# Two feed-forwards of a transformer: the up projections by seven block products in place of eight

## The chip, the cores and the metric

One core of a Trainium2 chip runs the whole kernel. The metric is the device time of one execution in microseconds (us), the median of several runs. A core has five engines that work side by side, each through its own list of instructions in order: TensorE (PE: matmuls into PSUM, with a weight load PEld ahead of each), VectorE (DVE), ScalarE (ACT), GpSimd (POOL) and SyncE (SP, which issues most loads from memory here). They wait for one another by semaphores.

## The reference

A model of two layers over 512 latent and 256 context tokens of width 1024, in float32. Layer 0 mixes by attention, layer 1 by a gated recurrent scan (HGRN); after each mixer comes a feed-forward. Layer 0's runs over all 768 tokens, layer 1's over the 512 latent ones only.

```python
def modulate(h, shift, scale):
    return h * (1.0 + scale) + shift

def swiglu(h, w_in, w_out):          # w_in 1024 x 5632, w_out 2816 x 1024
    a, u = jnp.split(h @ w_in, 2, axis=-1)
    return (jax.nn.silu(a) * u) @ w_out

# per layer; shift, scale and gate come from ada_w[i], six chunks of 1024 columns
h = h + gt1_l * mixer(modulate(rms_norm(h, norm_mix_w[i]), sh1_l, sc1_l))
h = h + gt2_l * swiglu(modulate(rms_norm(h, norm_ffn_w[i]), sh2_l, sc2_l), ffn_w_in[i], ffn_w_out[i])
```

## The kernel before

Tokens stand in the columns, features in the 128 partitions: `hT` is eight tiles of 128 x 768. Every float32 product is done in three passes of a rounded format (`mm3`): `split` makes of each operand a rounded high part (a cast on ACT) and the rest as a low part (a subtraction on VectorE, in a few places on POOL); TensorE then does high by high, high by low and low by high into the same PSUM tile.

A feed-forward (`ffn`) goes through the 2816 hidden features in 22 pairs of tiles: 128 columns of the a half and 128 of the u half of `w_in`. For each, `chain` loads a raw weight tile (128 x 1024, 512 KB, four buffers `raw`), splits it into `whi` and `wlo` (three buffers each), and runs eight contraction tiles by three passes over the tokens: in layer 0 a matmul of 512 and one of 258 columns each time, in layer 1 one of 256 and one of 258. The two extra columns carry the modulation's shift, for the tokens go in not yet normalised: only `hT` times a column `a_c` is split into `fnh` and `fnl`. Each token's reciprocal root of its mean square (`rst`) is found meanwhile by `token_scale`, and multiplied into the product afterwards by `scaled`, which reads PSUM and writes `ta` or `tu`; `hidden` then makes silu(a) x u of them and splits it into `gh` and `gl`. After 8, 7 and 7 pairs (`PARTS`) the down projection runs over what is there and adds the result to `hT` (`residual`, the `hT<-ffo` operations).

The reciprocal root: squares on ACT are added up, `rstd_cols` sums them over the features by small matmuls and takes the power -1/2 on POOL, `rstd_psum` turns the columns into a row in PSUM, by diagonal blocks `dg` on VectorE and a matmul that broadcasts.

Between these steps `fill.step` puts pieces of other work: the modulation of a later stage (`ada_ffn`, `ada_acc`), which multiplies weight rows by the conditioning vector on VectorE (`adacc<-adw`) while it streams 512 KB tiles. In layer 0 that is chunk 5 of layer 0, then all six of layer 1. The order of each engine's list is fixed when the program is built, by the order in which the code is written and by a scheduler of the framework; at run time engines only wait.

The stages of the profiled execution: preparation to about 184 us, attention to 437.5, feed-forward 0 from 439 to about 1019, the scan to about 1497, feed-forward 1 to the end.

## Time and profile before

| | us |
|---|---|
| median of 3 runs (1899.4 to 1904.18) | 1900.67 |
| profiled execution | 1901.45 |
| its span | 1899.4 |
| TensorE busy | 1833.4 (97%) |
| VectorE busy | 1127.6 (59%) |
| ScalarE busy | 680.3 (36%) |
| GpSimd busy | 394.8 (21%) |

The mean granted TensorE clock was 0.988 of full speed. In the rows of the profile, L106 is line 106 of the kernel; `out<-in` names the tiles an instruction writes and reads; `<-` behind a number of idle time names who ended the wait. Groups give the busy total, the mean duration in ns, and the idle time ahead of them. Rows of a timeline begin with the start and the duration.

### The profile page before, as it was taken

Reading aid. Unit: us, or ns where it says so; the run is one execution under the profiler, and the core shown is the slowest. Engines: PE = TensorE matmul, PEld = TensorE weight load, DVE = VectorE, ACT = ScalarE, POOL = GpSimd, SP = SyncE. Lnnn points to the kernel's source line nnn. Section 1 sums busy time; section 2 is a strip of 40 time slices with the busy share of each in tenths; the row PEclk is TensorE's granted clock in tenths of the full one; section 3 lists DMA queues with packets and bytes.
Section 4 is the critical chain, followed back from the end, with each engine's and each line's share of the span. In section 5 each row is a group of like instructions: output and inputs, shape, how many; then the busy total and the mean of one; then the engine's idle time right before and its main releaser. Section 6 shows DMA issues by size and latency. Waiting matters only on the chain. (4 is left out here: it accounts for less than half of the span.)

```text
span 1899.4 us, 29674 instructions
## 1 busy us (share of the span) xinstructions
PE 1833.4 (97%) x12111; PEld 1633.3 (86%) x12111; DVE 1127.6 (59%) x1821; ACT 680.3 (36%) x1222; POOL 394.8 (21%) x401
## 2 busy tenths in 40 slices
PE   8989999998999999999998989999998999999998
PEld 6778788887888888888887979889897799898997
DVE  3676788888866446445545555564647744344444
ACT  3333877763321122112224423233333432222224
POOL 1243534532000000000002444354436100000000
PEclk9989999998999999999999999999999999999999
DMA  9433200012424235353321211111111133333331
GB/s 325 169 104 100 100 2 23 23 46 78 155 89 133 79 93 174 88 154 107 100 66 51 79 45 45 57 56 56 56 56 45 45 93 97 89 89 98 92 88 57
DMA packets 206152, 166.37 MB, mean 88 GB/s; under 512 B 6801, under 2 KB 189249, under 8 KB 206017
## 3 DMA queue, kind: packets, MB, share of 16 engines
q1 hardware_dynamic: 205728, 163.43, 28.1%
q8 instruction: 96, 1.57, 0.3%
q10 hardware_dynamic: 288, 1.05, 0.1%
q14 instruction: 40, 0.32, 0.1%
HBM read 162.36 MB, written 2.10 MB: 87 GB/s over the span
## 5 line engine op out<-in xcount | busy, mean ns | idle before, releaser
L106 PE MATMUL ffi<-fnl,whi_fi 128*128 128x258 f32 (+2 forms) x1408 | 439.5, 312 | 2.6 <-DVE fnl L781 2.6
L105 PE MATMUL ffi<-fnh,whi_fi 128*128 128x258 f32 (+2 forms) x1408 | 440.3, 313 | 1.4 <-ACT fnh L780 1.3
L107 PE MATMUL ffi<-fnh,wlo_fi 128*128 128x258 f32 (+2 forms) x1408 | 437.5, 311 | 0.0
L106 PEld LDWEIGHTS ffi<-fnl,whi_fi 128*128 128x128 f32 x1408 | 268.2, 190 | 19.3 <-DVE fnl L781 3.6
L105 PEld LDWEIGHTS ffi<-fnh,whi_fi 128*128 128x128 f32 x1408 | 266.8, 190 | 18.0 <-ACT fnh L780 1.5
L107 PEld LDWEIGHTS ffi<-fnh,wlo_fi 128*128 128x128 f32 x1408 | 267.2, 190 | 15.9
L82 ACT CAST whi_fi<-raw_fi 128x1024 fp32r<-128x1024 f32 x88 | 92.3, 1050 | 359.0 <-issue 190.3
L250 POOL TENSOR_TENSOR rc<-rc,mhalf 128x2 f32<-128x2 f32 (+2 forms) x6 | 6.4, 1068 | 929.0 <-DVE rc L248 929.0
L105 PE MATMUL ffo<-gh,whi_fo 128*128 128x512 f32 (+1 forms) x542 | 192.2, 355 | 0.9 <-DVE modc L206 0.5
L107 PE MATMUL ffo<-gh,wlo_fo 128*128 128x512 f32 (+1 forms) x542 | 190.8, 352 | 0.0
L106 PE MATMUL ffo<-gl,whi_fo 128*128 128x512 f32 (+1 forms) x542 | 190.7, 352 | 0.0
L646 DVE SCALAR_TENSOR_TENSOR hT<-ffo,modc,hT 128x512 f32<-128x512 f32 (+1 forms) x74 | 47.8, 648 | 128.7 <-PE ffo L107 128.6
L222 DVE SCALAR_TENSOR_TENSOR adacc<-adw,csil,adacc 128x1024 f32<-128x1024 f32 x70 | 88.3, 1280 | 57.5 <-DMA adw<-in_ada_w_dram 57.3
L82 ACT CAST whi_fo<-raw_fo 128x896 fp32r<-128x896 f32 (+1 forms) x48 | 47.0, 980 | 202.5 <-PE ffo L106 98.5
L105 PEld LDWEIGHTS ffo<-gh,whi_fo 128*128 128x128 f32 x542 | 101.9, 188 | 16.8 <-issue 1.5
L106 PEld LDWEIGHTS ffo<-gl,whi_fo 128*128 128x128 f32 x542 | 101.9, 188 | 15.4
L107 PEld LDWEIGHTS ffo<-gh,wlo_fo 128*128 128x128 f32 x542 | 101.8, 188 | 15.3
L1103 POOL TENSOR_TENSOR KD<-KD,tot 128x384 f32<-128x384 f32 x96 | 100.3, 1068 | 68.7 <-ACT kc L1086 67.1
L85 DVE TENSOR_TENSOR wlo_fi<-raw_fi,whi_fi 128x1024 fp32r<-128x1024 f32 x87 | 106.1, 1221 | 7.5 <-ACT whi_fi L82 6.5
L660 POOL TENSOR_SCALAR pf<-pf,st 128x768 f32<-128x768 f32 (+1 forms) x96 | 73.7, 769 | 119.3 <-DVE st L659 75.5
L85 DVE TENSOR_TENSOR ptl<-pt,pth 128x384 fp32r<-128x384 f32 (+1 forms) x160 | 79.5, 522 | 9.7 <-ACT pth L82 8.4
L1103 DVE TENSOR_TENSOR QD<-QD,tot 128x256 f32<-128x256 f32 x96 | 56.3, 626 | 42.2 <-PE lv L1096 42.0
(315 smaller groups left out, 4203.2 us busy)
## 6 DMA issues: line engine op xcount, KB each, us to landing
raw_fi<-in_ffn_w_in_dram SPq DMA_DIRECT2D x88, 512.0 KB, 3.8
adw<-in_ada_w_dram SPq DMA_DIRECT2D x80, 512.0 KB, 4.3
raw_fo<-in_ffn_w_out_dram SPq DMA_DIRECT2D x32, 448.0 KB, 3.6
raw_fo<-in_ffn_w_out_dram SPq DMA_DIRECT2D x16, 512.0 KB, 3.8
raw_hz<-in_hgrn_w_in_dram SPq DMA_DIRECT2D x14, 512.0 KB, 3.8
adr<-in_ada_w_dram SPq DMA_DIRECT2D x16, 256.0 KB, 4.5
adr<-in_ada_w_dram SPq DMA_DIRECT2D x8, 512.0 KB, 7.0
raw_wq<-in_attn_w_qkv_dram SPq DMA_DIRECT2D x8, 512.0 KB, 5.5
```

The source lines that it names most:

```text
L82: ACT.copy(hi, src)
L85: (eng or DVE).tensor_tensor(lo, src, hi.bitcast(F32), op=ALU.subtract)
L105: PE.matmul(ps, ahi, bhi, start=first, stop=False)
L106: PE.matmul(ps, ahi, blo, start=False, stop=False)
L107: PE.matmul(ps, alo, bhi, start=False, stop=last)
L222: DVE.scalar_tensor_tensor(a, raw, cc, a, op0=ALU.mult, op1=ALU.add)
L250: POOL.tensor_tensor(rc, rc, mhalf.to_broadcast([P, nt]), op=ALU.pow)
L646: DVE.scalar_tensor_tensor(hT[o][:, a:e], ps, mcol(layer, ch, o, v), hT[o][:, a:e], op0=ALU.mult, op1=ALU.add)
L660: POOL.tensor_scalar(pf, pf, st3[:, 2:3], 1.0, op0=ALU.mult, op1=ALU.mult)
L1103: eng.tensor_tensor(view, view, f, op=ALU.mult)
```

## The change

With the features of w_in split into two halves of 512, the a and u tiles of a pair form a 2 x 2 block matrix, and the tokens' halves of features and of tokens another. The changed kernel forms their product with Winograd's variant of Strassen's method: seven products of blocks (`b11`, `b21`, `t1`, `t2`, `t3`, `t4`, `b22` are the token-side operands) instead of eight, each over four contraction tiles, three passes, and half of the tokens: 384 columns in layer 0, 256 in layer 1. That is 84 matmuls a pair.

The weights' sums and differences are made for each pair by POOL (`sums`, four operations of 128 x 512, in place on the raw tiles and in `sw`, of which there is one buffer). A pair then has four groups to split: g0 and g1 (1024 wide), g2 (512) and g3 (1024), in place of two of 1024. The products gather in three PSUM tiles X, Y and Z; ACT copies c11, c12 and c22 out of X as it grows, since further products are added onto it, VectorE adds Z and Y to them, ACT does the silu of c11 and c12, and the gating products go to VectorE (c11 with X, which is in PSUM) and POOL (c12 with c22). The order of TensorE is p1, p2 of pair j, pe3 of pair j-1, then pe1, pe2 of pair j; each group is split two steps before it is used.

The tokens are normalised ahead of the projection: the reciprocal root is multiplied in on VectorE (`xhalf`), the shift added on ACT, and the token-side differences are taken (twelve operations on POOL, four on VectorE, in place in `x`). For layer 0 the sum of squares is taken along with attention's last output projection. `scaled`, `rst` and the two extra columns go. Layer 0 gets five parts (5, 5, 4, 4, 4 pairs) instead of three; layer 1 keeps 8, 7 and 7.

The modulation's chunk 5 of layer 0 moves from VectorE in feed-forward 0 to TensorE in attention; layer 1's is done in halves of 512 columns with three steps a pair.

```diff
-PARTS = [(0, 8), (8, 7), (15, 7)]
+PARTS = [
+    [(0, 5), (5, 5), (10, 4), (14, 4), (18, 4)],
+    [(0, 8), (8, 7), (15, 7)],
+]
+NJ = HID // P
...
+    def mm3(ps, ahi, alo, bhi, blo, first, last, onto=False):
+        kw = dict(skip_group_check=True) if onto else {}
+        PE.matmul(ps, ahi, bhi, start=first, stop=False, **kw)
+        PE.matmul(ps, ahi, blo, start=False, stop=False, **kw)
+        PE.matmul(ps, alo, bhi, start=False, stop=last, **kw)
...
+    def ada_acc(layer, ch, hf, nv, fp):
+        c0 = ch * D + hf * 512
+        accs = [fp.tile([P, 512], F32, tag=f"adacc{v}", name=f"adacc{layer}{ch}{hf}{v}") for v in range(nv)]
...
+            if g == KVH - 1:
+                sumsq_add(acc, ap_, hT[o], o, o == 0)
+        if g == KVH - 1:
+            rcs[0] = rstd_cols(cst, [acc], T)
...
-    pfill.add(ada_chunk(4, None, lambda: ap_.tile([P, T], F32, tag="pf", bufs=4, name="arows"), ring_raw))
+    for ch in (4, 5):
+        pfill.add(ada_chunk(ch, None, lambda: ap_.tile([P, T], F32, tag="pf", bufs=4, name="arows"), ring_raw))
...
-        for k in range(KT):
-            if pre is not None:
-                next(pre, None)
-            for v, a, e, off in cols:
-                ac = a_c[:, k, v : v + 1]
-                ACT.activation(hi[k][:, a + off : e + off], hT[k][:, a:e], AF.Copy, scale=ac)
-                DVE.scalar_tensor_tensor(lo[k][:, a + off : e + off], hT[k][:, a:e], ac,
-                                         hi[k][:, a + off : e + off].bitcast(F32), op0=ALU.mult, op1=ALU.subtract)
...
-            rc = rstd_cols(fp, [acc_n[:, :n]], n)
-            yield
-            psr = rstd_psum(fp.tile([P, T + 2], F32, tag="ta", bufs=2, name="dg"), rc, n)
-            for v, a, e, off in cols:
-                ACT.copy(rst[:, a + off : e + off], psr[v])
-            yield
-
...
+        def group(key, src):
+            w = src.shape[1]
+            hi = ring.tile([P, 1024], F32R, tag="whi", bufs=3, name=f"whi_{key}")[:, :w]
+            lo = ring.tile([P, 1024], F32R, tag="wlo", bufs=3, name=f"wlo_{key}")[:, :w]
+            split(hi, lo, src)
+            G[key] = (hi, lo)
+
+        def sums(j):
+            wa, wu = W[j]
+            a11, a12, a21, a22 = wa[:, 0:512], wa[:, 512:1024], wu[:, 0:512], wu[:, 512:1024]
+            sw = fp.tile([P, 1024], F32, tag="sw", name=f"sw{j}")
+            POOL.tensor_tensor(sw[:, 512:1024], a21, a22, op=ALU.add)
+            POOL.tensor_tensor(sw[:, 0:512], sw[:, 512:1024], a11, op=ALU.subtract)
+            POOL.tensor_tensor(a11, a11, a21, op=ALU.subtract)
+            POOL.tensor_tensor(a21, a12, sw[:, 0:512], op=ALU.subtract)
+            W[j].append(sw)
+
+        def split0(j):
+            group(f"g0{j}", W[j][0])
+
+        def split1(j):
+            group(f"g1{j}", W[j][2])
+
+        def split2(j):
+            group(f"g2{j}", W[j][0][:, 0:512])
+
+        def split3(j):
+            group(f"g3{j}", W.pop(j)[1])
...
+        def prod(ps, key, off, x, first):
+            hi, lo = G[key]
+            xh, xl = xops[x]
+            for k in range(4):
+                c = slice(off + k * P, off + (k + 1) * P)
+                mm3(ps, hi[:, c], lo[:, c], xh[:, k], xl[:, k], first and k == 0, k == 3, not first)
...
+        def p1(j):
+            prod(S[j]["X"], f"g0{j}", 0, "b11", True)
+            S[j]["c11"] = ctile("c11", j)
+            ACT.copy(S[j]["c11"], S[j]["X"])
+
+        def p2(j):
+            prod(S[j]["Z"], f"g0{j}", 512, "b21", True)
+            c = S[j]["c11"]
+            DVE.tensor_tensor(c, S[j]["Z"], c, op=ALU.add)
+            ACT.activation(c, c, AF.Silu)
+
+        def pe1(j):
+            prod(S[j]["X"], f"g1{j}", 0, "t2", False)
+            S[j]["c12"] = ctile("c12", j)
+            ACT.copy(S[j]["c12"], S[j]["X"])
+            prod(S[j]["Y"], f"g1{j}", 512, "t1", True)
+
+        def pe2(j):
+            prod(S[j]["X"], f"g2{j}", 0, "t3", False)
+            c = S[j]["c22"] = ctile("c22", j)
+            ACT.copy(c, S[j]["X"])
+            DVE.tensor_tensor(c, S[j]["Y"], c, op=ALU.add)
+
+        def pe3(j):
+            prod(S[j]["Y"], f"g3{j}", 0, "b22", False)
+            c = S[j]["c12"]
+            DVE.tensor_tensor(c, S[j]["Y"], c, op=ALU.add)
+            ACT.activation(c, c, AF.Silu)
+            prod(S[j]["X"], f"g3{j}", 512, "t4", False)
+
+        gh, gl = {}, {}
+
+        def hidden(j):
+            p_, jj = next((p_, j - j0) for p_, (j0, nj) in enumerate(parts) if j0 <= j < j0 + nj)
+            gh[j] = fp.tile([P, n], F32R, tag=f"gh{jj}", name=f"gh{p_}_{jj}")
+            gl[j] = fp.tile([P, n], F32R, tag=f"gl{jj}", name=f"gl{p_}_{jj}")
+            st = S.pop(j)
+            DVE.tensor_tensor(st["c11"], st["X"], st["c11"], op=ALU.mult)
+            POOL.tensor_tensor(st["c12"], st["c12"], st["c22"], op=ALU.mult)
+            split(gh[j][:, 0:H], gl[j][:, 0:H], st["c11"])
+            split(gh[j][:, H:n], gl[j][:, H:n], st["c12"])
...
+            fill.step(3)
...
-                for k in range(KT):
-                    for o_, a, e in msp:
-                        mm3(ps[:, o_ : o_ + e - a], whi[:, k], wlo[:, k], hi[k][:, a:e], lo[k][:, a:e],
-                            k == 0, k == KT - 1)
...
+                add(split0_sums, zero)
+                if not prev:
+                    def three(j=j):
+                        pe3(j - 1)
+                        hidden(j - 1)
+                    add(lambda j=j: split3(j - 1), three)
+                add(lambda j=j: split1(j), lambda j=j: pe1(j))
+                add(lambda j=j: split2(j), lambda j=j: pe2(j))
...
+        pss = rstd_psum(fp.tile([P, n], F32, tag=f"gl{nmax - 1}", name="dg"), rc, n)
+        tags = [f"gh{i}" for i in range(nmax)] + [f"gl{i}" for i in range(nmax - 1)]
+        x = [fp.tile([P, n], F32, tag=tags[k], name=f"x{k}") for k in range(KT)]
+
+        def xhalf(k, half):
+            for v, a, e in halves[half]:
+                r = pss[a // 512][:, a % 512 : a % 512 + e - a]
+                DVE.scalar_tensor_tensor(x[k][:, a:e], hT[k][:, a:e], a_c[:, k, v : v + 1], r,
+                                         op0=ALU.mult, op1=ALU.mult)
+                ACT.activation(x[k][:, a:e], x[k][:, a:e], AF.Identity, bias=mcol(layer, 3, k, v))
...
+        for i in range(4):
+            xhalf(i, 0)
+            xsplit("b11", i, x[i][:, 0:H])
+        for j in range(2):
+            p1(j)
+        for i in range(4):
+            xhalf(4 + i, 0)
+            xsplit("b21", i, x[4 + i][:, 0:H])
+        for j in range(2):
+            p2(j)
+        split1(0)
+        sums(1)
+        for i in range(4):
+            xhalf(i, 1)
+            xhalf(4 + i, 1)
+            b11, b12, b21, b22 = x[i][:, 0:H], x[i][:, H:n], x[4 + i][:, 0:H], x[4 + i][:, H:n]
+            DVE.tensor_tensor(b11, b12, b11, op=ALU.subtract)
+            xsplit("t1", i, b11)
+            POOL.tensor_tensor(b11, b22, b11, op=ALU.subtract)
+            xsplit("t2", i, b11)
+        pe1(0)
+        split1(1)
+        for i in range(4):
+            b11, b12, b21, b22 = x[i][:, 0:H], x[i][:, H:n], x[4 + i][:, 0:H], x[4 + i][:, H:n]
+            POOL.tensor_tensor(b12, b22, b12, op=ALU.subtract)
+            xsplit("t3", i, b12)
+        pe1(1)
+        split2(0)
+        pe2(0)
+        split2(1)
+        for i in range(4):
+            b11, b12, b21, b22 = x[i][:, 0:H], x[i][:, H:n], x[4 + i][:, 0:H], x[4 + i][:, H:n]
+            xsplit("b22", i, b22)
+            POOL.tensor_tensor(b21, b21, b11, op=ALU.subtract)
+            xsplit("t4", i, b21)
+        split3(0)
+        pe2(1)
+        pe3(0)
+        hidden(0)
+        done = loaded = 0
+        for i, (_, pe_fn) in enumerate(seq):
+            while done < min(i + 3, len(seq)):
+                while loaded < len(loads) and loads[loaded][0] <= done + 2:
+                    loads[loaded][1]()
+                    loaded += 1
+                seq[done][0]()
+                done += 1
+            pe_fn()
...
-    ffn(0, False, lambda fill, fp: fill.add(ada_ffn(0, 5, fp)), ada_last, tail=norm_tail)
+    ffn(0, False, ada_last, rc=rcs[0], tail=norm_tail)
```

How this moves the instructions. **VectorE in feed-forward 1**, a pair before (the low parts `wlo_fi` of two weight tiles, the scaling `ta` and `tu` from PSUM, the gating, and the low part `gl`):

```order
L835 TENSOR_TENSOR ta<-ffi,rst 128x256
L836 TENSOR_TENSOR ta<-ffi,rst 128x258
L85 TENSOR_TENSOR wlo_fi_9_1_15638<-raw_fi_9_1_15636,whi_fi_9_1_15637 128x1024
L835 TENSOR_TENSOR tu<-ffi,rst 128x256
L836 TENSOR_TENSOR tu<-ffi,rst 128x258
L865 SCALAR_TENSOR_TENSOR tu<-tu,ta 128x512
L85 TENSOR_TENSOR wlo_fi_10_0_15693<-raw_fi_10_0_15691,whi_fi_10_0_15692 128x1024
L85 TENSOR_TENSOR gl_0_15454<-tu,gh_0_15447 128x512
```

and after. Here raw_fi_16604 and raw_fi_16606 are the a and u tiles of one pair, j; 16474 and 16476 those of j-1, 16733 and 16735 those of j+1:

```order
L870 TENSOR_TENSOR c_16730<-yy,c_16730 128x256
L857 TENSOR_TENSOR c_16755<-xz,c_16755 128x256
L89 TENSOR_TENSOR wlo_g_16772<-raw_fi_16604,whi_g_16771 128x512
L875 TENSOR_TENSOR c_16700<-yy,c_16700 128x256
L886 TENSOR_TENSOR c_16625<-xz,c_16625 128x256
L89 TENSOR_TENSOR wlo_g_16810<-raw_fi_16733,whi_g_16809 128x1024
L89 TENSOR_TENSOR gl_3_16802<-c_16625,gh_3_16801 128x256
L89 TENSOR_TENSOR gl_3_16802<-c_16700,gh_3_16801 128x256
L89 TENSOR_TENSOR wlo_g_16845<-raw_fi_16606,whi_g_16844 128x1024
L89 TENSOR_TENSOR wlo_g_16868<-sw_16813,whi_g_16867 128x1024
```

In order: c22 of j-1, c11 of j, the low part of g2 of j, c12 of j-1, the gating of j-1, the low part of g0 of j+1, the two halves of gl of j-1, the low parts of g3 of j and of g1 of j+1 (sw). Buffers of the u tile of j-1 (16476) are taken by that of j+1 (16735) once g3 of j-1 has been split.

**ACT in the same period**, where before only two weight casts, a silu and the gh cast stood:

```order
L869 COPY c_16730<-xz 128x256
L852 COPY c_16755<-xz 128x256
L86 CAST whi_g_16771<-raw_fi_16604 128x512
L858 ACTIVATE c_16755<-c_16755 128x256
L876 ACTIVATE c_16700<-c_16700 128x256
L86 CAST whi_g_16809<-raw_fi_16733 128x1024
L86 CAST gh_3_16801<-c_16625 128x256
L86 CAST gh_3_16801<-c_16700 128x256
L863 COPY c_16830<-xz 128x256
L86 CAST whi_g_16844<-raw_fi_16606 128x1024
L86 CAST whi_g_16867<-sw_16813 128x1024
```

The copy of c12 of pair j (c_16830, read from xz, the X tile) stands behind the second gh cast, which reads c_16700, the product that POOL makes; the cast of g3 (raw_fi_16606) stands behind the copy.

**POOL in the same period**, which before had nothing in a pair of feed-forward 1:

```order
L812 TENSOR_TENSOR raw_fi_16604<-raw_fi_16604,raw_fi_16606 128x512
L813 TENSOR_TENSOR raw_fi_16606<-raw_fi_16604,sw_16683 128x512
L810 TENSOR_TENSOR sw_16813<-raw_fi_16735 128x512
L811 TENSOR_TENSOR sw_16813<-sw_16813,raw_fi_16733 128x512
L887 TENSOR_TENSOR c_16700<-c_16700,c_16730 128x256
L812 TENSOR_TENSOR raw_fi_16733<-raw_fi_16733,raw_fi_16735 128x512
L813 TENSOR_TENSOR raw_fi_16735<-raw_fi_16733,sw_16813 128x512
```

The product c_16700 of pair j-1 stands between the second and third sum of pair j+1, and so behind the landing of that pair's weights.

**VectorE in feed-forward 0 after, at pairs 3 and 4**, where the modulation's operations of 512 columns (`adacc`) come between low parts (`wlo_g`) and the sums from PSUM:

```order
L209 TENSOR_SCALAR adacc_6563<-adw_6565,csil 128x512
L209 TENSOR_SCALAR adacc_6564<-adw_6565,csil 128x512
L211 SCALAR_TENSOR_TENSOR adacc_6563<-adw_6609,csil,adacc_6563 128x512
L211 SCALAR_TENSOR_TENSOR adacc_6564<-adw_6609,csil,adacc_6564 128x512
L89 TENSOR_TENSOR wlo_g_6111<-raw_fi_5860,whi_g_6110 128x1024
L211 SCALAR_TENSOR_TENSOR adacc_6563<-adw_6655,csil,adacc_6563 128x512
L89 TENSOR_TENSOR wlo_g_6134<-sw_6079,whi_g_6133 128x1024
L870 TENSOR_TENSOR c_6126<-yy,c_6126 128x384
L211 SCALAR_TENSOR_TENSOR adacc_6564<-adw_6655,csil,adacc_6564 128x512
L211 SCALAR_TENSOR_TENSOR adacc_6563<-adw_6697,csil,adacc_6563 128x512
L211 SCALAR_TENSOR_TENSOR adacc_6564<-adw_6697,csil,adacc_6564 128x512
L857 TENSOR_TENSOR c_6151<-xz,c_6151 128x384
```

Before, they were 1024 wide and half as many, and stood between two low parts of 1024 a pair; now they stand between four low parts, and pairs 2, 3, 4 and 9 hold 10 to 12 of them, pair 8 holds 8, others 3 to 5.

279 lines of the change are left out of this document (145 added, 134 removed).

## The prediction

> **What bounds the kernel now.** First I read the page's busy times and its 40 slices (each digit the busy tenths of 1/40 of the span), then a table of stages.
>
> ```profile
> PE 1833.4 (97%) x12111; PEld 1633.3 (86%) x12111; DVE 1127.6 (59%) x1821; ACT 680.3 (36%) x1222; POOL 394.8 (21%) x401
> ...
> PE   8989999998999999999998989999998999999998
> ...
> POOL 1243534532000000000002444354436100000000
> ```
>
> TensorE is busy in every slice and POOL does almost nothing in the two feed-forwards (slices 11 to 21 and 32 to 40). The table says the same by stage; 439 to 1019 is feed-forward 0 (768 tokens), 1497 to 1899 feed-forward 1 (512), and the short stretches are their entrances (PEclk is the granted clock).
>
> ```profile
> core 0: us, PE busy (x) PEld busy (x) DVE busy (x) ACT busy (x) POOL busy (x), PEclk, DMA share, GB/s
> 184.00:437.00 253.00, 245.16 (x1700) 214.75 (x1697) 208.36 (x466) 183.88 (x429) 107.08 (x115) 1.00 0.13 42
> 439.00:1019.00 580.00, 572.50 (x3250) 498.03 (x3250) 337.74 (x396) 137.69 (x197) 17.76 (x8) 0.99 0.36 110
> 1497.00:1899.00 402.00, 392.28 (x2778) 366.58 (x2777) 185.22 (x269) 125.01 (x164) 7.28 (x6) 0.99 0.29 87
> 435.00:439.00 4.00, 1.87 (x11) 1.19 (x9) 1.62 (x6) 1.77 (x3) 0.65 (x1) 1.00 0.00 0
> 439.00:445.00 6.00, 4.54 (x13) 3.36 (x14) 6.00 (x9) 6.00 (x13) 1.72 (x1) 0.53 0.30 87
> 460.00:465.00 5.00, 2.82 (x17) 2.48 (x15) 4.62 (x4) 1.05 (x1) 0.55 (x1) 0.82 0.80 237
> 465.00:470.00 5.00, 5.00 (x18) 4.42 (x19) 2.52 (x9) 0.00 (x0) 2.27 (x1) 0.50 0.31 98
> 1493.00:1497.00 4.00, 3.01 (x13) 1.73 (x12) 3.24 (x5) 0.66 (x1) 1.21 (x3) 1.00 0.22 65
> 1497.00:1500.00 3.00, 2.22 (x10) 1.53 (x9) 1.96 (x5) 0.69 (x1) 0.00 (x0) 1.00 0.44 130
> ```
>
> Both feed-forwards are bound by TensorE (98.7% and 97.6% busy), VectorE is at 58% and 46%. So a matmul saved there is time saved, as long as nothing else needs longer than the shortened TensorE.
>
> **Part 1, the matmuls.** The records' durations overlap, so I take distances between starts.
>
> ```profile
> 699.87 0.40 PE L105 MATMUL ffi<-fnh,whi_fi 128*128 128x512 f32 x1
> ...
> 700.57 0.28 PE L105 MATMUL ffi<-fnh,whi_fi 128*128 128x258 f32 x1
> ...
> 1699.76 0.28 PE L105 MATMUL ffi<-fnh,whi_fi 128*128 128x256 f32 x1
> ...
> 1700.96 0.28 PE L106 MATMUL ffi<-fnl,whi_fi 128*128 128x258 f32 x1
> ```
>
> Three matmuls of 512 columns take 0.70 us, 0.233 each; ten of 256 or 258 take 1.20 us, 0.120 each. Half-way, 384 columns cost 0.177 us (bounds: the 0.120 and 0.233 of its neighbours).
> - Feed-forward 0, a pair of tiles: before 48 x (0.233 + 0.120) = 16.9 us; after 7 products x 4 x 3 = 84 matmuls of 384: 14.8. 22 pairs: -46.
> - Feed-forward 1: before 96 x 0.120 = 11.5; after 84 x 0.120 = 10.1. 22 pairs: -32.
> - Chunk 5 of layer 0's modulation moves to TensorE in attention: 32 narrow matmuls at up to the 0.12 of 256 columns, on a stage that is 97% TensorE: 3.8 at most, 0 if they fall into its gaps; I take +2.5.
>
> The down projections keep their matmuls. Cutting feed-forward 0's into five parts adds 16 VectorE updates of `hT`, which fall under TensorE work. Sum so far: -75.5.
>
> **Part 2, what POOL and VectorE get.** Prices (busy total, mean ns):
>
> ```profile
> L85 DVE TENSOR_TENSOR wlo_fi<-raw_fi,whi_fi 128x1024 fp32r<-128x1024 f32 x87 | 106.1, 1221 | 7.5 <-ACT whi_fi L82 6.5
> L85 DVE TENSOR_TENSOR gl<-tu,gh 128x512 fp32r<-128x512 f32 x44 | 30.1, 685 | 5.8 <-ACT gh L82 5.8
> L85 DVE TENSOR_TENSOR gl<-tu,gh 128x256 fp32r<-128x256 f32 x22 | 9.2, 417 | 0.0
> L82 ACT CAST whi_fi<-raw_fi 128x1024 fp32r<-128x1024 f32 x88 | 92.3, 1050 | 359.0 <-issue 190.3 <-PE ffi L106 81.3 <-PE ffo L106 67.8
> L82 ACT CAST gh<-tu 128x256 fp32r<-128x256 f32 x22 | 8.8, 402 | 0.0
> L1020 ACT COPY v<-hv 128x256 f32<-128x256 f32 x24 | 8.8, 371 | 35.0 <-PE hv L107 35.0
> L660 POOL TENSOR_SCALAR pf<-pf,st 128x256 f32<-128x256 f32 x32 | 15.4, 483 | 33.9 <-PE pt L670 19.5 <-DVE st L659 12.5 <-PE rx L641 1.4
> L1103 POOL TENSOR_TENSOR KD<-KD,tot 128x384 f32<-128x384 f32 x96 | 100.3, 1068 | 68.7 <-ACT kc L1086 67.1 <-DVE tot L1110 1.6
> 116.57 1.29 POOL L496 TENSOR_TENSOR qrot<-qhat,wq 128x512 f32<-128x512 f32 x1 [2.19 <-DVE qhat L492]
> raw_fi<-in_ffn_w_in_dram SPq DMA_DIRECT2D x88, 512.0 KB, 3.8
> ```
>
> A weight sum of 512 columns is 1.29 us on POOL; the 256-column product between 0.48 and 1.07, taken as 0.73. Per pair of feed-forward 1 POOL has 4 x 1.29 + 0.73 = 5.9 us, VectorE's subtractions 3 x 1.22 + 0.69 + 2 x 0.42 = 5.2, ACT under 7. Each alone is below 10.1. But POOL and VectorE get in each other's way:
>
> ```profile
> 453.27 2.49 POOL L238 TENSOR_TENSOR acc_o<-acc_o,sq 128x768 f32<-128x768 f32 x1 [0.96 <-ACT sq L237]
> 453.98 2.60 DVE L238 TENSOR_TENSOR acc_n<-acc_n,sq 128x768 f32<-128x768 f32 x1
> 1131.26 2.45 POOL L1103 TENSOR_TENSOR KD<-KD,tot 128x384 f32<-128x384 f32 x2 [0.78 <-ACT kc L1086]
> 1131.80 2.19 DVE L1103 TENSOR_TENSOR QD<-QD,FB 128x256 f32<-128x256 f32 x2
> ```
>
> The two QD operations, 256 columns from SBUF like the 0.42 us `gl`, took 1.10 each while POOL's KD ran; which is a KD and a QD in turn, not side by side; `acc_n` needed 2.60 beside `acc_o`. So two-operand VectorE work out of SBUF and POOL work take turns, and their sum counts: 11.1 us a pair, about 10.6 as a waiting operation starts up meanwhile.
>
> The Trainium skill, "SBUF — State Buffer", section "SBUF: two separate sides", says that GpSimd and a VectorE operation with two SBUF inputs share a port pair under an exclusive lock, so that the loser waits for the whole instruction. The trace agrees (the QD rows). It speaks against this change: by the rule alone a pair takes the full 11.1, +22 over 22 pairs, where 10.6 gives +11; neither goes into the sum, which the next paragraph makes from a longer wait.
>
> Above that stands a loop through the queues, read off the order in feed-forward 1: the subtraction of g3 of pair j-1 frees a raw buffer; the load of pair j+1 lands after 3.8; POOL does its first two sums (2.58) and then the product of pair j-1 (0.73); ACT's gh cast waits for that (0.40), and behind it stand the copy of c12 (0.37), without which TensorE can't go on to pe2, and the cast of g3 (1.05); then comes its subtraction (1.22). That is one period: 10.15 us, some 10.5 with hand-overs. VectorE's g0 subtraction, in turn with the two sums, and a third sum ahead of g3's subtraction each add up to 1.2 to 1.3: 10.5 to 13.0, of which I take the middle, 11.8. The excess over 10.1 is 1.7 in some 17 of 22 periods (next to a down projection TensorE has other work): **+29** (+7 to +49).
>
> Feed-forward 0 has 14.8 us to hide the same loop (about +0.5 for wider operations), POOL at 5.2 + 1.1 and VectorE at 5.5 of port work. Layer 1's modulation comes on top, in 512-column pieces of about 0.68 (the `gl` row); with 3 a pair it fits: 13.8. The order bunches them, though: 10 or 11 in each of pairs 2, 3 and 4, 8 in pair 8, 12 in pair 9, so 18 to 20 us in turn against 14.8. **+15** (0 to +30): 3 to 5 us for each of the four fullest, a little less than that as splits run two steps ahead.
>
> **Part 3, the entrances.** Before, tokens scaled by a column go into TensorE at once (last two rows); the reciprocal root and its broadcast come later:
>
> ```profile
> L250 POOL TENSOR_TENSOR rc<-rc,mhalf 128x2 f32<-128x2 f32 (+2 forms) x6 | 6.4, 1068 | 929.0 <-DVE rc L248 929.0
> L258 DVE TENSOR_SCALAR dg<-ident,rc 128x128 f32<-128x128 f32 x16 | 7.8, 541 | 3.9 <-POOL rc L250 3.9
> 437.39 0.28 PE L107 MATMUL wos<-qT,wlo_wo 128*128 128x256 f32 x1
> 438.95 0.90 PE L105 MATMUL ffi<-fnh,whi_fi 128*128 128x512 f32 x2 [1.28 <-ACT fnh L780]
> ```
>
> Feed-forward 0's entrance loses 2.1 + 1.5 + 2.2 of idle time (435 to 439, 439 to 445, 460 to 465) and, at 0.53, 0.82 and 0.50 of the clock, 2.1 + 0.5 + 2.5 of what was busy, and a little between: about 12. Feed-forward 1's loses 1.0 + 0.8 from 1493 to 1500 and something beyond, at most 4. After, the normalisation stands ahead: the last square 0.6, the sum 0.7, the column sums 0.5, the power 1.1, six diagonal blocks at 0.54, the broadcast 0.3, the first x scaled, shifted and split 1.9 (estimates, but for the two rows): 8.3 us with TensorE idle, and 6.9 with the four blocks and narrower tiles of feed-forward 1. Then POOL and VectorE in turn: 28 low parts and 4 differences on VectorE (at 0.55 between the `gl` rows, or 0.42), 12 differences on POOL (1.0, or 0.73), the sums of pair 1 (5.2), and the splits left of pairs 0 and 1 (3.8); 38.6 us, or 31.3, less some 1.6 for start-ups. TensorE has 25.4 and 17.1 us of its own for that time (two pairs without the last product of the second). Losses 8.3 + 37.0 - 25.4 = 20 and 6.9 + 29.7 - 17.1 = 19.5, so **+8** and **+15** against before (0 to +20 each: below 0 the operands would have to be ready at once).
>
> **The sum.** -46 - 32 + 2.5 + 29 + 15 + 8 + 15 = -8.5. Against the profiled execution's own 1901.45 (span 1899.4): 1893; the median of the runs, 1900.67, is 0.8 lower: **1892 us**. No change shows as anything within 0.3% (5.7 us): the three runs lie between 1899.4 and 1904.18.
>
> **The rivals.**
> - *TensorE sets the pace throughout* (the gain is kept). For: each engine alone has time in hand, the `KD` operations take 1.07 on average against 1.22 in the colliding row, so that not all collide, and the loop's lower bound is near 10.1. Against: the turns alone are 10.6. With the loop at +7, the bunches at +5 and the entrances at +10 together it is -75.5 + 22, or 1847; with the entrances as above 1860. 0.30.
> - *The loop runs at its worst, slower.* In feed-forward 1, each period has both collisions, 13.0 us: +49, and the sum is +11.5 (1912). The place is the copy of c12 behind gh on ACT; it decides from a period of 12.3 on, where all losses together equal the gain. If VectorE's modulation in feed-forward 0 also sits ahead of `c12` there and makes the ordinary pair 15.8, it is +17 more: 1929. 0.36.
> - *A halved clock.* The stretch with 2.18 us idle in five (460 to 465) was followed by one at clock 0.50, which lost 2.5 us. Stalls of 3 to 5 us in four bunched pairs would each bring that too, +10; if the stalls of feed-forward 1 fell in one piece in half of its periods, 11 x 2.5 = +27: 1902 to 1929. It is in the case above, as its longer end. The Trainium skill, "TensorE: Matmul & The Clock Gate", Part 1, puts the drop after an idle window of about 3.4 us; by that rule the 1.7 us stalls of feed-forward 1 do nothing. The trace shows it after 2.2 us, so I keep the case.
> - *The change doesn't do what it says*: a 384-column matmul at 0.233 gives 84 x 0.233 = 19.6, +59 in place of -46, near 1998. The steps from 256 to 512 are even, so 0.02.
>
> **Chances.** The forecast, from 1880 to 1906, has 0.32: 0.13 of it faster, 0.16 the same, 0.03 slower, as its centre lies near the bound. TensorE's pace has 0.30, all faster. The slow loop has 0.36: 0.34 slower, 0.02 the same. The matmul that is no shorter has 0.02. In all faster 0.43, the same 0.18, slower 0.39. The range leaves a tenth at each end: from 1850, near the first rival, to 1934, just above the second.
>
> **What would show it.** In the after profile: `ffi` replaced by products with starts 0.177 and 0.120 apart (part 1); POOL from 4% to over 40% in both feed-forwards; sums well over 1.29 us and subtractions well over 1.22 where they overlap; in feed-forward 1 TensorE idle about 1.7 us in a period of 11.8, ended by ACT's copy of c12 or VectorE's low parts; pairs 2 to 4 and 9 of feed-forward 0 longer by 3 to 5; idle time of some 20 us after the last `wos` and the last `hwo` matmul. TensorE above 97% in feed-forward 1 would make the forecast wrong to the fast side; a period above 12.5 to the slow side.

## The result and the profile after

The changed kernel takes 1956.43 us (median of 4 runs, 1953.43 to 1958.79) against 1901.45 for the kernel before in the same session: 1.0287 times, 95% interval 1.0264 to 1.0310. It is slower by 55 us, and lies beyond the upper end of the forecast range. Of the runs further down, one execution of e8_gh_late_dve took 4389 us and is left out of its median.

The page after (busy times, two of the 40-slice rows):

```profile
PE 1807.2 (93%) x11689; PEld 1617.5 (83%) x11689; DVE 1330.0 (68%) x2106; ACT 828.0 (42%) x1572; POOL 704.9 (36%) x636
...
PE   8989999996899999999998999999998689999998
...
POOL 1243444434422413131303353443544454143340
```

TensorE is busy for 26 us less, and yet the span is 52 us longer: two dips stand where the feed-forwards begin (slices 10 and 32), and POOL now works through both. The table of stretches, as before (the entrances are 443 to 503 and 1525 to 1571):

```profile
core 0: us, PE busy (x) PEld busy (x) DVE busy (x) ACT busy (x) POOL busy (x), PEclk, DMA share, GB/s
443.00:458.00 15.00, 7.42 (x31) 5.98 (x32) 10.90 (x17) 4.79 (x7) 5.55 (x6) 0.66 0.01 2
458.00:503.00 45.00, 36.95 (x149) 29.70 (x150) 42.74 (x67) 30.70 (x66) 23.17 (x19) 0.77 0.14 42
503.00:573.00 70.00, 61.88 (x333) 58.76 (x333) 65.41 (x78) 27.32 (x45) 27.33 (x19) 0.98 0.36 106
...
1525.00:1571.00 46.00, 30.59 (x172) 26.59 (x171) 38.20 (x71) 26.87 (x63) 20.87 (x19) 0.78 0.12 35
1571.00:1658.00 87.00, 75.98 (x584) 73.84 (x583) 65.27 (x71) 43.92 (x80) 45.62 (x35) 0.96 0.31 89
...
1705.00:1785.00 80.00, 72.70 (x565) 70.10 (x565) 59.88 (x65) 40.25 (x72) 37.80 (x28) 0.98 0.29 86
...
1827.00:1896.00 69.00, 63.79 (x483) 61.57 (x482) 49.92 (x55) 34.15 (x62) 31.72 (x24) 0.95 0.29 84
```

In the pairs after feed-forward 0's entrance (503 to 573) VectorE is busy 93% of the time and TensorE 88%; in feed-forward 1's first part (1571 to 1658) TensorE has 11 us of idle time, where before it had almost none there. By stage, from the starts of its matmuls (us):

| | attention ends | feed-forward 0 | scan | feed-forward 1 | of it, entrance 0 / 1 |
|---|---|---|---|---|---|
| before | 437.4 | 577.9 | 491.7 | 384.9 | |
| after | 443.6 | 589.7 | 491.8 | 419.0 | 59.1 / 45.7 |

Attention ends with the last `wos` matmul. Feed-forward 0 is counted from there to the last `ffo` one of layer 0, the scan from there to the last `hwo`, feed-forward 1 from there to the last `fin`, and an entrance from the start of its stage to the first product of the third pair. The changes (+6.2, +11.8, +0.1, +34.2) make up the 52.

What the pairs of feed-forward 1 wait for, by the first rows of TensorE's waits from 1571 to 1896 (total, times, longest):

```profile
PE xz L110 <- ACT c L863: 18.4, 11, 2.2
PE xz L110 <- ACT c L852: 3.2, 1, 3.2
```

L863 is the copy of c12. One period of the loop that the prediction names, in rows of the timeline after (start, duration):

```profile
1737.39 1.36 POOL L813 TENSOR_TENSOR raw_fi<-raw_fi,sw 128x512 f32<-128x512 f32 x1
1737.52 2.32 DVE L89 TENSOR_TENSOR wlo_g<-raw_fi,whi_g 128x1024 fp32r<-128x1024 f32 x1
1739.86 3.72 SPq L795 DMA_DIRECT2D raw_fi<-in_ffn_w_in_dram  x2
1743.80 1.30 POOL L810 TENSOR_TENSOR sw<-raw_fi 128x512 f32<-128x512 f32 x1 [5.05 <-DVE c L875]
1745.18 1.29 POOL L811 TENSOR_TENSOR sw<-sw,raw_fi 128x512 f32<-128x512 f32 x1
1746.44 1.70 POOL L887 TENSOR_TENSOR c<-c,c 128x256 f32<-128x256 f32 x1
1748.17 0.41 ACT L86 CAST gh<-c 128x256 fp32r<-128x256 f32 x1 [2.63 <-POOL c L887]
1748.48 0.37 ACT L863 COPY c<-xz 128x256 f32<-128x256 f32 x1
1748.75 1.05 ACT L86 CAST whi_g<-raw_fi 128x1024 fp32r<-128x1024 f32 x1
1749.83 2.24 DVE L89 TENSOR_TENSOR wlo_g<-raw_fi,whi_g 128x1024 fp32r<-128x1024 f32 x1
```

The low part of g3 ends at 1739.84 and the load is issued at 1739.86; the next such low part ends at 1752.07: a period of 12.23 us. (The load landed at 1743.58. The first sum started at 1743.80, and its row names a step of VectorE that ended at 1743.74, so the two ended almost together here.) Its links are those of the prediction; two of them collide: the product takes 1.70 instead of 0.75, and the low part, which starts in the middle of a POOL sum, 2.24 instead of 1.22. The first two rows show the turn: the sum ends at 1738.75, and 1.09 us later the low part is done, as if it had begun there.

### The profile page after: what moved, and what is told of

Same layout as the page of the kernel before. It is cut to its first block, busy times and chain, and to the rows that moved or that the text cites. A ratio compares the mean times of both kernels' runs of the same rounds, so it can differ in the third digit from the quotient of the medians.

```text
span 1951.7 us, 30199 instructions
## 1 busy us (share of the span) xinstructions
PE 1807.2 (93%) x11689; PEld 1617.5 (83%) x11689; DVE 1330.0 (68%) x2106; ACT 828.0 (42%) x1572; POOL 704.9 (36%) x636
## 4 chain that ended last, share of the span: by engine, by line
PE 57%; DVE 17%; DMA 9%; POOL 6%; issue 6%; ACT 5%; SPq 0%; POOLq 0%; DVEq 0%; ACTq 0%
DMA adw<-in_ada_w_dram 6%; PE ffo L110 5%; PE ffo L112 5%; PE ffo L111 5%; PE xz L110 3%; DVE wlo_g L89 3%; DVE adacc L211 3%; PE xz L112 3%; PE xz L111 3%; PE pt L673 2%; PE lv L1270 2%; DMA raw_fi<-in_ffn_w_in_dram 2%; PE hz L110 2%; PE hz L111 2%; PE hz L112 2%
## 5 line engine op out<-in xcount | busy, mean ns | idle before, releaser
L89 DVE TENSOR_TENSOR wlo_g<-raw_fi,whi_g 128x1024 fp32r<-128x1024 f32 (+1 forms) x132 | 175.0, 1326 | 35.6 <-ACT whi_g L86 33.7
L86 ACT CAST whi_g<-raw_fi 128x1024 fp32r<-128x1024 f32 (+1 forms) x132 | 119.4, 906 | 147.5 <-PE xz L111 94.1
L810 POOL TENSOR_TENSOR sw<-raw_fi 128x512 f32<-128x512 f32 x44 | 61.4, 1395 | 280.4 <-DMA raw_fi<-in_ffn_w_in_dram 193.4
L211 DVE SCALAR_TENSOR_TENSOR adacc<-adw,csil,adacc 128x512 f32<-128x512 f32 x112 | 104.0, 944 | 45.6 <-DMA adw<-in_ada_w_dram 45.5
L86 ACT CAST whi_fo<-raw_fo 128x512 fp32r<-128x512 f32 (+3 forms) x64 | 50.0, 782 | 160.7 <-PE ffo L111 139.7
L887 POOL TENSOR_TENSOR c<-c,c 128x384 f32<-128x384 f32 (+1 forms) x44 | 50.3, 1144 | 180.7 <-ACT c L876 180.7
L812 POOL TENSOR_TENSOR raw_fi<-raw_fi,raw_fi 128x512 f32<-128x512 f32 x44 | 63.1, 1433 | 125.8 <-issue 73.8
L89 DVE TENSOR_TENSOR ptl<-pt,pth 128x384 fp32r<-128x384 f32 (+1 forms) x160 | 79.8, 524 | 11.6 <-ACT pth L86 10.4
L86 ACT CAST pth<-pt 128x384 fp32r<-128x384 f32 (+1 forms) x160 | 69.8, 461 | 35.3 <-PE pt L673 23.5
L659 DVE TENSOR_REDUCE st<-sc 128x1 f32<-128x768 f32 (+1 forms) x96 | 74.2, 773 | 15.3 <-PE sc L619 12.5
L89 DVE TENSOR_TENSOR gl<-c,gh 128x384 fp32r<-128x384 f32 (+1 forms) x88 | 78.6, 919 | 4.4 <-ACT gh L86 4.2
```

The costliest lines, as they stand in the source:

```text
L86: ACT.copy(hi, src)
L89: (eng or DVE).tensor_tensor(lo, src, hi.bitcast(F32), op=ALU.subtract)
L211: DVE.scalar_tensor_tensor(a, raw, cc, a, op0=ALU.mult, op1=ALU.add)
L659: DVE.tensor_reduce(st3[:, 0:1], ps[:, :nk], op=ALU.max, axis=AX.X, negate=True)
L810: POOL.tensor_tensor(sw[:, 512:1024], a21, a22, op=ALU.add)
L812: POOL.tensor_tensor(a11, a11, a21, op=ALU.subtract)
```

## The experiments

Sizes of stages in the runs that keep all of the work, and in those that leave some out (us, as in the table above). "Period" is the mean distance from the first matmul of a pair of feed-forward 1 to that of the next, over the 12 distances that hold just the 84 matmuls of a pair; before, with 96, it was 11.45. The expectations average over 15 distances, some with more or fewer matmuls, and so have 12.6 for the changed kernel where the table has 12.3.

| | total | attention ends | feed-forward 0 | feed-forward 1 | entrance 0 / 1 | period |
|---|---|---|---|---|---|---|
| after | 1956.4 | 443.6 | 589.7 | 419.0 | 59.1 / 45.7 | 12.3 |
| e1_gh_late | 1943.7 | 444.6 | 591.8 | 406.3 | 60.7 / 45.8 | 11.4 |
| e2_sums_dve | 1893.2 | 445.2 | 559.0 | 388.1 | 59.6 / 44.6 | 10.6 |
| e4_no_ada | 1918.3 | 443.2 | 551.5 | 418.3 | 59.1 / 47.3 | 12.3 |
| e8_gh_late_dve | 1892.9 | 444.0 | 564.6 | 383.2 | 61.1 / 45.0 | 10.3 |
| e9_no_norm | 1953.9 | 444.5 | 591.4 | 416.8 | 60.8 / 43.6 | 12.4 |
| e10_no_chunk5 | 1952.0 | 436.4 | 593.7 | 422.5 | 62.8 / 45.9 | 12.2 |
| e12_sums_dve_no_ada | 1883.8 | 445.0 | 546.4 | 390.5 | 58.7 / 44.3 | 10.8 |
| e14_no_lows | 1888.8 | 443.9 | 556.9 | 387.3 | 57.8 / 43.4 | 10.6 |
| e16_no_lows_dve | 1881.3 | 445.1 | 552.0 | 384.3 | 50.8 / 40.6 | 10.6 |
| e13_best | 1887.1 | 443.1 | 558.0 | 383.4 | 58.5 / 44.8 | 10.4 |
| e15_hybrid | 1889.0 | 444.5 | 561.3 | 384.9 | 60.2 / - | - |

**The loop, taken apart (e1_gh_late).** `issue_after` holds the two gh casts back in ACT's list:

```diff
-                    def three(j=j):
-                        pe3(j - 1)
-                        hidden(j - 1)
+                def two(j=j, held=not prev):
+                    pe2(j)
+                    if held:
+                        hidden(j - 1, casts.get(j))
...
+            with tc.issue_after(after.ins) if after is not None else ExitStack():
                 split(gh[j][:, 0:H], gl[j][:, 0:H], st["c11"])
```

> Only the order of ACT's list changes: the two gh casts of pair j-1, the second of which waits for POOL's product, are issued behind the copy of c12 and the cast of g3 of pair j, instead of ahead of them. Theory 1 (the loop: freed raw buffer, landing, two sums, product, gh cast, copy of c12, cast and low part of g3, freed buffer): with the product out of the loop the period of feed-forward 1, 12.6 us on average over 15 plain pairs, falls to the turns of POOL and VectorE, 10.6 to 11.1; 15 x 1.7 = -25 there, -3 in feed-forward 0, total about 1928. Theory 2 (the turns themselves already take 12 us and more, because each waits for whole instructions of the other): the period stays at 12 or above and the total within 8 us of 1956.

Measured: 1943.69 us, ratio to before 1.0224 (1.0209 to 1.0239). The period falls from 12.3 to 11.4, and feed-forward 1 by 12.7 us; feed-forward 0 doesn't get shorter. That is half of what theory 1 says, and more than theory 2 allows: the loop holds the pairs at 12.3, and behind it something holds them at 11.4. TensorE's wait for the copy of c12 is gone; the first row of its waits is now the copy of c11 (this kernel's L855), which waits itself for a low part of VectorE, `gl` (a row of the timeline of e1_gh_late, behind its waits). As `gl` is one of the operations that the edit moves back, part of what holds the pairs at 11.4 can be of its own making.

```profile
PE xz L112 <- ACT c L855: 13.2, 15, 3.2
```

```profile
1725.53 0.37 ACT L855 COPY c<-xz 128x256 f32<-128x256 f32 x1 [1.61 <-DVE gl L90]
```

**The sums to VectorE (e2_sums_dve).**

```diff
-            POOL.tensor_tensor(sw[:, 512:1024], a21, a22, op=ALU.add)
+            DVE.tensor_tensor(sw[:, 512:1024], a21, a22, op=ALU.add)
```

and so for the other three of `sums`.

> The four weight sums of each pair move from POOL to VectorE, nothing else. A 512-column operation of VectorE with two operands took 0.69 us (gl), on POOL 1.29 alone and 1.40 on average here, so the work that takes turns falls from 11.1 to about 8.7 us a pair in feed-forward 1, and the loop loses 1.2 us and its collisions. If the port is what stretches the pairs (theories 1 and 2): periods of 10.3 to 10.8 in feed-forward 1, -25 to -35; in feed-forward 0 -5 to -15; total 1908 to 1925. If VectorE's own load counts (rival: with the sums it has about 10.1 us a pair in feed-forward 1 and 13 to 18 in feed-forward 0 against TensorE's 10.1 and 14.6): periods near 11.5 to 12.5, pairs 2 to 4 of feed-forward 0 slower than now, total 1950 or more.

Measured: 1893.20 us, ratio 0.9961 (0.9946 to 0.9975): 63 us less than after, and 7 less than before. More than forecast: feed-forward 0 gives 31, feed-forward 1 31. The period is 10.6, 0.3 above the 10.3 at which TensorE is busy all the time (e8_gh_late_dve below), though VectorE has 2.8 us more work a pair. The rival falls. Groups of after, then of e2_sums_dve (total busy, mean ns), show what VectorE had lost:

```profile
L89 DVE TENSOR_TENSOR wlo_g<-raw_fi,whi_g 128x1024 fp32r<-128x1024 f32 x88 | 138.8, 1578 | 33.5 <-ACT whi_g L86 33.2
L89 DVE TENSOR_TENSOR gl<-c,gh 128x256 fp32r<-128x256 f32 x44 | 41.6, 962 | 4.2 <-ACT gh L86 4.2
L89 DVE TENSOR_TENSOR gl<-c,gh 128x384 fp32r<-128x384 f32 x44 | 37.1, 877 | 0.2
L811 POOL TENSOR_TENSOR sw<-sw,raw_fi 128x512 f32<-128x512 f32 x44 | 67.3, 1530 | 3.3
L211 DVE SCALAR_TENSOR_TENSOR adacc<-adw,csil,adacc 128x512 f32<-128x512 f32 x112 | 104.0, 944 | 45.6 <-DMA adw<-in_ada_w_dram 45.5
```

```profile
L89 DVE TENSOR_TENSOR wlo_g<-raw_fi,whi_g 128x1024 fp32r<-128x1024 f32 x88 | 108.3, 1231 | 20.7 <-ACT whi_g L86 20.1
L89 DVE TENSOR_TENSOR gl<-c,gh 128x256 fp32r<-128x256 f32 x44 | 19.2, 468 | 0.8 <-ACT gh L86 0.8
L89 DVE TENSOR_TENSOR gl<-c,gh 128x384 fp32r<-128x384 f32 x44 | 22.9, 549 | 1.0 <-ACT gh L86 0.9
L811 DVE TENSOR_TENSOR sw<-sw,raw_fi 128x512 f32<-128x512 f32 x44 | 30.1, 684 | 0.3
L211 DVE SCALAR_TENSOR_TENSOR adacc<-adw,csil,adacc 128x512 f32<-128x512 f32 x112 | 84.0, 760 | 27.7 <-DMA adw<-in_ada_w_dram 27.7
```

The same operations on the same tiles took 30.5 + 22.4 + 14.2 + 20.0 = 87 us longer beside POOL's sums. The sum in the rows costs 1.53 us on POOL there and 0.68 on VectorE. The Trainium skill, "SBUF — State Buffer", section "SBUF: two separate sides", has this as an exclusive lock. The first two rows of the period above agree: the low part that started beside a sum was done 1.09 us after the sum's end.

**Without layer 1's modulation (e4_no_ada, and e12_sums_dve_no_ada on top of e2).** `ada_last` sets `modc[1]` to 0.01 instead of adding the six chunks.

> Leaves out layer 1's modulation in feed-forward 0 (its 96 loads of 256 KB, VectorE's adacc work, the adc matmuls); the modulation vectors are set to a constant. Theory A (feed-forward 0 is late because the modulation's VectorE work and loads stand between the low parts): feed-forward 0's excess outside its entrance, 48 us over the matmuls' own time, falls to about 10, total about 1918. Rival (feed-forward 0 is held by the same loop and turns as feed-forward 1, whatever the modulation): it falls by 10 at most, about 4 of it the adc matmuls, total above 1943.

> e2_sums_dve with layer 1's modulation left out of feed-forward 0 as in e4_no_ada. With the sums on POOL leaving it out was worth 38 us. If the modulation was dear because its VectorE work stood in turn with POOL: worth only 10 to 16 here (down projections 11, of it the adc matmuls), total 1877 to 1883. Rival (it costs by its VectorE time and loads as such): worth 30 or more, total below 1863.

Measured: 1918.26 us (ratio 1.0096, 1.0080 to 1.0113) and 1883.80 (0.9912, 0.9897 to 0.9926). The modulation costs feed-forward 0 38 us with the sums on POOL, as theory A says, and 9 in the total (13 in the stage) with them on VectorE, a little less than forecast. So most of it isn't dear as such: 112 + 16 operations of 512 columns nearly fit under TensorE's time as long as they don't also wait for POOL.

**All on VectorE (e8_gh_late_dve).** e1 and e2 together, with the c12 product and the token-side differences on VectorE too.

> All three at once: gh casts behind the copy of c12 and the cast of g3, and the weight sums, the c12 product and the twelve token-side differences on VectorE; POOL is free in both feed-forwards. If port turns and loop are the loss: feed-forward 1 at 10.3 to 10.6 a pair, entrances 5 to 8 us shorter each (12 differences at 0.55 or 0.42 instead of 1.0 or 0.73, no turns), feed-forward 0 outside the modulation's bunches at TensorE's 14.6: 1895 to 1910. If VectorE becomes the bound (10.5 us a pair in feed-forward 1): no better than e2_sums_dve, 1920 or more.

Measured: 1892.88 us, 0.9956 (0.9940 to 0.9973), 2 us below the forecast. Feed-forward 1 is 5 us shorter than in e2 and at TensorE's pace, a pair in 10.3 us (from 1804.67 to 1815.00 TensorE is busy for the whole 10.33); feed-forward 0 is 6 longer; the entrances don't shorten at all, which the forecast had wrong.

**What the entrances wait for (e9_no_norm).**

```diff
-                DVE.scalar_tensor_tensor(x[k][:, a:e], hT[k][:, a:e], a_c[:, k, v : v + 1], r,
-                                         op0=ALU.mult, op1=ALU.mult)
+                DVE.tensor_scalar(x[k][:, a:e], hT[k][:, a:e], a_c[:, k, v : v + 1], None, op0=ALU.mult)
```

> Leaves out the normalisation of the tokens: x is hT times its column, so nothing waits for the sum of squares, the power, the diagonal blocks and the broadcast (they still run). The entrance theory (normalising ahead leaves TensorE idle for 14 us in feed-forward 0 and 13 in feed-forward 1 between the last matmul of the mixer and the first product): each entrance is 8 to 11 us shorter, total 1935 to 1941. Rival (the making of the seven operands sets the entrance and the chain runs beside it): less than 4 us each, total above 1948.

Measured: 1953.93 us, 1.0277 (1.0261 to 1.0293), 2.5 less than after. The forecast's number fails and the rival's holds, but the run can't tell the two theories apart, for the chain still stands in the engines' lists. In feed-forward 0 all but two of the x operations stood behind the diagonal blocks in VectorE's list, and the first product comes 12.6 us after the last `wos` one (14.2 after). In feed-forward 1 the first two matmuls of the first product start 0.2 us after the last `hwo` one, and the rest wait behind the chain's own matmuls:

```profile
1527.87 0.79 PE L110 MATMUL xz<-xb11h,whi_g 128*128 128x256 f32 x2
1531.26 1.87 PE L248 MATMUL ssq<-ones,acc_n 128*128 128x2 f32 x8 [2.60 <-DVE acc_n L241]
...
1534.93 2.04 PE L262 MATMUL rstd<-dg,ones 128*128 128x128 f32 x8 [0.74 <-DVE dg L261]
1536.63 0.77 PE L110 MATMUL xz<-xb11h,whi_g 128*128 128x256 f32 x2
```

The third pair starts at 43.6 instead of 45.7. In every other run with seven products too, 12 to 16 us of each entrance pass before the first product starts; what an entrance without that chain would take stays open.

**Which work of theirs (e14_no_lows, e16_no_lows_dve).** `xsplit` casts only the high part, and `prod` uses it for both passes; e16 also moves the twelve differences from POOL to VectorE.

> e2_sums_dve without the low parts of the seven token-side operands: the 28 subtractions on VectorE at each entrance are left out, and the products use the high part in place of the low one, so that TensorE's work is the same. If VectorE's work on the operands sets the entrance (28 x 0.55 = 15.4 us in feed-forward 0, 28 x 0.42 = 11.8 in feed-forward 1, against some 20 and 16 us that TensorE waits there): the entrances are 11 to 15 and 8 to 12 us shorter, total 1866 to 1874. Rival (ACT's casts and shifts, or the chain of waits from operand to operand, set it): less than 5 us each, total above 1884.

> e14_no_lows with the twelve token-side differences on VectorE as well, which there has room for them since it makes no low parts of the operands (left out, as in e14_no_lows). In e14_no_lows POOL made the differences one behind the other from 470 to 487 us, at 1.0 to 1.46 each, and the casts of t2 waited for them. If POOL's row of differences and VectorE's low parts are two bounds of the entrance, of which either alone is enough: now both are gone, and feed-forward 0's entrance is 5 to 10 us shorter than in e14_no_lows, feed-forward 1's 4 to 8; total 1871 to 1880. Rival (ACT sets it: 24 shifts, 28 casts, the weights' casts and PSUM copies, 31 us of work in 42): less than 3 us each, total 1884 or more.

Measured: 1888.80 us (0.9934, 0.9921 to 0.9948) and 1881.30 (0.9888, 0.9865 to 0.9912). Without the low parts alone the entrances are 1.7 and 1.2 us shorter than in e2: the theory that these low parts alone set them falls. The timeline of e14_no_lows shows what took their place in feed-forward 0: POOL's twelve differences in a row (the first and the last), in turn with modulation that the scheduler put into VectorE's free time. From 474 to 494 us there are 14 of its operations, where e2 has 3 in its entrance, so that this entrance was not freed of VectorE work:

```profile
470.46 1.00 POOL L1068 TENSOR_TENSOR x<-x,x 128x384 f32<-128x384 f32 x1 [17.81 <-DVE x L1060]
...
485.47 1.34 POOL L1077 TENSOR_TENSOR x<-x,x 128x384 f32<-128x384 f32 x1
```

```profile
477.54 2.90 DVE L211 SCALAR_TENSOR_TENSOR adacc<-adw,csil,adacc 128x512 f32<-128x512 f32 x2
```

With POOL's differences moved as well, feed-forward 0's entrance is 7.0 us shorter, inside the 5 to 10 of the expectation, and feed-forward 1's 2.7, below its 4 to 8; the total lies just above the expected 1871 to 1880. For feed-forward 0 this fits two bounds, VectorE's low parts and POOL's differences, of which either is enough; it isn't shown cleanly, as e16 has only 6 modulation operations in that entrance and a higher granted clock behind the first product (0.87, against 0.77 in e14). What holds feed-forward 1's at 40.6 stays open. There 12.7 us pass before the first product; in the 27.9 us after it ACT is busy for 22.5, and taking work off ACT wasn't tried.

**Attention (e10_no_chunk5).** Chunk 5 is left out and the gate set to 0.01.

> Leaves out layer 0's modulation chunk 5 in attention (its loads and the matmuls pa<-adw; the gate is a constant). If these matmuls are what makes attention end at 443.6 instead of 437.4: it ends within 1 us of 437.5 and the total is 6 us less, 1950. Rival (the sum of squares in the last output projection holds it up): attention still ends after 441, total above 1953.

Measured: 1952.01 us, 1.0265 (1.0251 to 1.0279). Attention ends at 436.4, 7 us earlier, so the chunk, its loads or its matmuls, is what lengthens it. Only 4.4 us arrive at the end: in the profiled execution feed-forward 0 takes 4 longer, with its entrance, and feed-forward 1 another 3.5.

**Versions.** e11_hybrid: sums on VectorE, gh late and four modulation steps a pair in layer 0, and the old function in layer 1 (which there takes the second of its three parts for the last, so that only layer 0 is read).

> A version to beat both: layer 0 by seven products with the sums on VectorE, gh casts late and four modulation steps a pair instead of three, layer 1 by the old function with eight products. e2_sums_dve had 388 us in feed-forward 1 against 385 before, and some 10 us of modulation left in feed-forward 0's down projections: 1883 to 1890. Rival (four steps a pair overload VectorE, 11 + 2.7 us a pair of 14.6, and stretch the pairs): 1892 or more.

Measured: 1895.11 us. Layer 0 takes 567.2 us from the last `wos` to the last `ffo` matmul, against 559.0 with three steps and early gh casts in e2. So four steps a pair with late gh casts don't pay; which of the two costs the 8 us isn't shown, as e8_gh_late_dve, with late casts, three steps and POOL's other work on VectorE too, has 564.6.

e15_hybrid has e2's layer 0 and the old layer 1; e13_best has both layers changed, with POOL free in layer 1 only:

```diff
+        SIDE = DVE if layer else POOL
-            POOL.tensor_tensor(st["c12"], st["c12"], st["c22"], op=ALU.mult)
+            SIDE.tensor_tensor(st["c12"], st["c12"], st["c22"], op=ALU.mult)
```

> Layer 0 as in e2_sums_dve, layer 1 by the old function with eight products. If feed-forward 1 gains nothing from seven products, because the 1.2 us saved a pair go into its entrance: 1889 to 1891 (385 in place of 388 us in that stage). Rival (seven products are worth their matmuls there, 26 us over 22 pairs): 1910 or more.

> Each layer takes what was best for it: sums on VectorE in both; in layer 1 also the c12 product and the token-side differences on VectorE and the gh casts late. Feed-forward 0 as in e2_sums_dve (559 us from the last wos matmul to the last ffo one), feed-forward 1 as in e8_gh_late_dve (383): about 1888, 12 under before. Rival (the parts are not additive, since the order of the lists is made anew): 1893 or more.

Measured: 1889.01 us, 0.9937 (0.9925 to 0.9950), and 1887.09 us, 0.9933 (0.9919 to 0.9946). Both as expected. e13_best beats the kernel before by 14 us and the changed one by 69; seven products in layer 1 are worth 1.5 us there (384.9 against 383.4): the 25 us that its pairs save went almost wholly into its entrance, which loses 44.8 - 17.1 = 28 us where before it lost 4.

## Why the prediction was wrong

It forecast -8.5 us; the span grew by 52.3. The step that failed most is the price of layer 1's modulation in feed-forward 0, which was charged to the fullest pairs alone and at VectorE's undisturbed durations; the two entrances together missed by as much. By its terms:

- *The matmuls (-46 and -32)*: from start to start 384 columns took 0.173 us (0.177 was forecast), 256 columns 0.120. Where nothing else holds it up, a pair takes 14.7 us in feed-forward 0 (e4_no_ada) and 10.3 in feed-forward 1 (e8_gh_late_dve), against 17.0 and 11.45 before. That makes -50 and -25: the second saving was put 7 us too high.
- *Attention (+2.5)*: +6.2, and 7.2 by e10. The step "32 narrow matmuls" failed: chunk 5 is 64 of them (the whole program has 384 matmuls `pa<-adw` before and 448 after).
- *The loop in feed-forward 1 (+29)*: right in mechanism, somewhat small. The late gh casts of e1 give back 12.7 us, the sums on VectorE (e2) 30.9, both together with the product and the differences on VectorE (e8) 35.8; as each edit alone also eases the other's wait, they don't add up. Some 8.5 us of it (an estimate: the missing clock of the rows above, 0.04 x 87 + 0.02 x 80 + 0.05 x 69) is a lower granted clock, which is 1.00 in the same stretch of e1 and e8.
- *The modulation's bunches in feed-forward 0 (+15)*: worth 38 us by e4, and 13 with the sums on VectorE (e12). The prediction put every pair outside the four fullest at nothing, since with 3 operations a pair "it fits: 13.8". But pairs 13 and 17, in whose time only 4 and 3 of them ran, took 17.6 and 17.3 us, hardly less than pair 3 with its 18.5, while e4 has 14.7 for each. The low parts and the modulation were stretched beside POOL everywhere (1.58 us instead of 1.23, 0.94 instead of 0.76), and TensorE waited for low parts, sums from PSUM and the updates of `hT`, all VectorE's (from 503 to 1000 us):

```profile
PE xz L112 <- DVE wlo_g L89: 8.2, 6, 2.1
PE yy L110 <- DVE c L870: 4.3, 4, 1.4
PE ffo L110 <- DVE hT L649: 4.1, 3, 2.1
```

- *The entrances (+8 and +15)*: 59.1 - 25 = 34 and 45.7 - 17.1 = 29 us lost, against 12 and at most 4 before: +22 and +25. Three things were missed. The 24 operations that scale x (0.61 us for 384 columns), about 11 us of VectorE in feed-forward 0, weren't in the sum of the operands' work. The chain ahead of the first product took 14.2 and 13.0 us, where 8.3 and 6.9 were estimated: in feed-forward 0 it took 3.7 us to the column sums instead of 1.3, the column sums took 2.3 instead of 0.5, and the six diagonal blocks 4.34 beside POOL's sums instead of 3.2:

```profile
443.56 0.28 PE L112 MATMUL wos<-qT,wlo_wo 128*128 128x256 f32 x1
447.28 2.31 PE L248 MATMUL ssq<-ones,acc 128*128 128x2 f32 x12 [3.45 <-DVE acc L241]
449.87 1.34 POOL L253 TENSOR_TENSOR rc<-rc,mhalf 128x6 f32<-128x6 f32 x1 [23.87 <-DVE rc L251]
451.25 4.34 DVE L261 TENSOR_SCALAR dg<-ident,rc 128x128 f32<-128x128 f32 x6 [1.46 <-POOL rc L253]
457.74 1.01 PE L110 MATMUL xz<-xb11h,whi_g 128*128 128x384 f32 x2 [1.30 <-ACT xb11h L86]
```

  And the 25.4 us of TensorE's own work were counted at full clock: from 458 to 503 TensorE is idle for only 8 us, but busy for 37 at a granted clock of 0.77. How much of an entrance the clock costs, and how much would be waited for anyway, no run separates.
- *The sum*: -50 - 25 + 6 + 36 + 38 + 22 + 25 = +52. That it meets the measured 52.3 so closely is chance, as the 36 and the 38 come from runs that move or leave out work, and the 38 is the whole of a modulation that the kernel before also had.
- *The rivals*: the slow loop, with its place on ACT behind gh, is the one that came closest; at 12.3 it wasn't at its worst, and what carried the time beyond its 1929 were the terms above. The halved clock was real, in the entrances (0.66 to 0.78) and five times in the pairs of feed-forward 1, each time behind a stall of 1.8 to 3.2 us; other stalls of that size passed without it. One of them is the stretch from 1724.36 to 1727.76, right behind a wait of 1.81 us for the copy of c12 (PEclk is the column ahead of the last two):

```profile
1724.36:1727.76 3.40, 3.40 (x19) 3.40 (x18) 2.94 (x3) 1.76 (x3) 1.64 (x2) 0.50 0.02 5
```

## What to carry to other kernels

When work moves to POOL to relieve other engines, count it together with VectorE's two-operand work out of SBUF (and with one-operand work like the diagonal blocks below), in every stage that it enters, and price each VectorE operation there at the stretched duration. Work that VectorE does in half the time can be cheaper there even when VectorE is the busier engine: here the kernel with the sums on VectorE took 63 us less. A saving per tile that needs operands made anew at a stage's start has to be set against that start: in feed-forward 1 an entrance of 45 us, with 17 us of TensorE's own work in it, gave back the saving of 22 pairs.
